# Start columns of the projection weights in their SBUF slots: by tile index instead of by kind

## The chip, the cores and the metric

The kernel runs on one core of one Trainium2 chip. The metric is device time in microseconds (us) for one launch; the time of a kernel is the median of its runs.

## The reference, cut to what matters

One layer of a hybrid block on 528 tokens (16 meta tokens and 512 real ones), width 2048, all in float32:

```python
hn = rmsnorm(h_res, norm_in_g)
P  = hn @ w_in                      # 2048 x 8320: the combined input projection
Pr, Pc = P[..., :4224], P[..., 4224:]
# Pr, after a token shift: r, k, v, g_r (1024 each) and two low-rank parts (64 each)
y  = delta-rule recurrence over 16 heads of 64 (r, decay, k, v, kk, kk*a)
y_a = (groupnorm(y) + bonus) * silu(g_r)
# Pc: Bg, Cg, hc, g_c (1024 each)
y_b = Bg * causal_conv3(Cg * hc) * silu(g_c)
out = rmsnorm(h_res + concat(y_a, y_b) @ w_out, norm_f_g)[:, 16:]
```

## The kernel before

**Projection.** The 8320 columns of `w_in` are 65 tiles of 128 columns. Each tile has a kind and an index: `lora` (one tile), `k`, `v`, `r`, `g`, `C`, `h`, `B`, `gc` (eight tiles each, index `i` from 0 to 7). `plan` (lines 152 to 159) lists them in the order in which they are computed. The products are made in three passes: activations and weights are each split into a high part in the matmul's reduced format (float32r) and the remainder as a low part, and every product is high x high, then weight-high x activation-low, then weight-low x activation-high. The activations lie in `xh` and `xl`, 16 rows (contraction blocks `kt`) of `LX` = 576 columns each. `steps` (L316 to L329) issues the matmuls: the weights are the stationary operand (128 columns, loaded for each matmul by a separate weight load) and `xh` or `xl` the moving one. The matmuls of all tiles stand on L326, except the first six (L485).

Which columns of the activations stream depends on the kind:

```python
FULL = ((0, 256), (256, L))      # lora, k, v:   256 and 272 columns, L = 528
TAIL = ((14, 272), (272, L))     # r, g, C, h:   258 and 256 columns
REAL = ((META, L),)              # B, gc:        512 columns, META = 16
```

So a tile of FULL or TAIL is 96 matmuls: for each of the four quarters of the contraction (`k4`), 12 of the first range (four `kt`, three passes each) and then 12 of the second. A tile of REAL is 48 matmuls of 512 columns.

**Weight slots.** A half row of a weight tile (1024 columns, 512 KB) is brought by a DMA into `raw`, and `split_w` (L136 to L140) makes two quarters of it: for each quarter ScalarE copies the high part (L138) and VectorE or GpSimd subtracts to give the low part (L139). `parts_of` (L128 to L131) takes a slot of `2 * 512 + 64` = 1088 columns from a pool with tag `hl` and six buffers, and puts the high part at start column `o` and the low part at `o + 512`; so up to 64 columns of a slot are free, and `o` says where in the slot the weights begin. Before, `o` is read from the table `SHIFT` (L78) by kind:

```python
SHIFT = {"lora": 16, "k": 16, "v": 16, "r": 32, "C": 64, "h": 32, "B": 16, "g": 32, "gc": 16, "out": 40}
```

`kind_of` (L133, L134) finds the kind of the tile that a quarter belongs to; the first four tiles are computed together, so their eight half rows stand interleaved.

**Where things lie.** In the built program the six slots begin at bytes 4128 + n x 4352 of a partition, `xh` at 42528 and `xl` at 79392. 4352 bytes are 17 x 256 and a row of `xh` is 2304 = 9 x 256, and all these places leave 32 when divided by 256. So the place of an operand's first column modulo 64 columns (256 bytes) is its column number alone: 0 and 0 for the two ranges of FULL, 14 and 16 for TAIL, 16 for REAL, and `o` for the weights, whatever the slot, the contraction block or the part.

**Order.** TensorE's order is written out by hand: the small matmuls of the recurrence (grams L674, triangular inverses L846 to L905, the chunk loop L947 to L1003) are set between projection matmuls by `fill`, which counts 0.43 ns per moving column and stops at hand-set amounts (`FW`). DMAs are put off by the same clock (`later`). After the last projection tile comes the output projection (L1236, and L1445 for its last piece), whose weights are the moving operand: they go through the same slots at start column 40 (`parts_of("out", ...)` in `split_unit`, L1204 to L1216).

Of the kernel before, what the change touches and what calls it, by code (L numbers as in the profile page):

```python
# [74 lines left out]


LX = 576
SHIFT = {"lora": 16, "k": 16, "v": 16, "r": 32, "C": 64, "h": 32, "B": 16, "g": 32, "gc": 16, "out": 40}  # L78


@with_exitstack
def hymba_kernel(ctx: ExitStack, tc: tile.TileContext, xt, xtok, front, w_in, w_out, pv, lup, cst, msk, gf, out):
# [27 lines left out]
    plan = [("lora", 0), ("k", 0), ("r", 0), ("B", 0), ("v", 0), ("k", 1), ("r", 1), ("v", 1), ("g", 0), ("g", 1)]  # L110
# [10 lines left out]
    N_IN = len(stream)  # L121
# [5 lines left out]

    def parts_of(kind, name):  # L128
        t = wp.tile([P, 2 * 512 + 64], F32R, tag="hl", name=name, bufs=6)
        o = SHIFT[kind]  # L130
        return t[:, o : o + 512], t[:, o + 512 : o + 1024]  # L131

    def kind_of(j):  # L133
        return "out" if j >= N_IN else plan[j % 4 if j < 8 else j // 2][0]  # L134

    def split_w(q, rq, eng):  # L136
        hi, lo = parts_of(kind_of(q // 2), f"w{q}")
        nc.scalar.copy(hi, rq)  # L138
        low[q] = eng.tensor_tensor(out=lo, in0=rq, in1=hi.bitcast(F32), op=ALU.subtract).ins  # L139
        quarters[q] = (hi, lo)  # L140
# [90 lines left out]
    for n in range(4):  # L231
        quarters[2 * n] = parts_of(kind_of(n), f"w{2 * n}")
    F0, F1, F2 = KT + P + L, 4 * P + L, 8 * P + 2 * L
    fr = [view("bt", F0), view("r0", 3 * P), view("bk", F1), view("gt0", F2)]
    o = 0
# [61 lines left out]
    with tc.issue_after(head):  # L297
        nc.vector.tensor_scalar(
            out=omm, in0=pvt[:, V_MU : V_MU + 33], scalar1=-1.0, scalar2=1.0, op0=ALU.mult, op1=ALU.add
        )  # L300
        for d, off in (
# [4 lines left out]
                out=d, in0=pvt[:, off : off + 8], scalar1=0.5, scalar2=None, op0=ALU.mult  # L306
            )
        nc.vector.tensor_scalar(
            out=hv[:, 4], in0=pvt[:, V_KA : V_KA + 8], scalar1=-0.5, scalar2=1.0, op0=ALU.mult, op1=ALU.add
# [854 lines left out]
    U = {unit: u for u, unit in enumerate(units)}  # L1164
# [34 lines left out]
    def split_unit(unit, t, home=None):  # L1199
        for q in range(2):  # L1200
            rq = t()[:, q * 512 : (q + 1) * 512]
            if home is None:
                hi, lo = parts_of("out", f"o{U[unit]}_{q}")
            else:  # L1204
                hi, lo = home[q]
            nc.scalar.copy(hi, rq)
            last = nc.vector.tensor_tensor(out=lo, in0=rq, in1=hi.bitcast(F32), op=ALU.subtract)  # L1207
            right[unit, q] = (hi, lo)
        if unit[:2] == (1, "M3"):
            last_low[unit[2]] = last.ins  # L1210

    def here(t, n):
        return xa[t][:, n * 512 : (n + 1) * 512] if n < 2 else xb[n - 2][:, t]
# [83 lines left out]
    def split_home(g):  # L1297
        f = ("S1", "S3", "S4", "S5")[g]
        tiles = [
            pw.tile([P, 4, HT], F32R, tag=f"{f}0{a}", name=f"home{g}{a}").rearrange("p a b -> p (a b)") for a in range(2)  # L1300
        ]
        split_unit(
            (1, "M2", g), passing(1, 1, 0, g),
            [(tiles[0][:, 512 * q : 512 * q + 512], tiles[1][:, 512 * q : 512 * q + 512]) for q in range(2)],
        )
# [7 lines left out]
    for half in range(2):  # L1313
        o = 28 * half
        for g in range(4):
            b = o + 4 + 4 * g
            if half == 0:
                if g == 3:
                    at(-1, begin_chain, 0, g)
                    at(0, split_unit, (0, "M1", g), chained(g))  # L1320
            else:
                at(o + g - 4, begin_chain, 1, g)
                at(o + g - 2, split_unit, (1, "M1", g), chained(g))
            at(max(o + g, b - 5), add_by_transfer, half, 0, 1, g)
            at(b - (6 if g else 5), request, half, 0, 1, g)
            at(b - (4 if g else 5), request, half, 1, 1, g)
            at(b - 2, split_unit, (half, "P5", g), chained(g))
            at(b - 1, add, passing(half, 0, 1, g), half, 1, 1, g)
            at(b - 1, split_unit, (half, "M7", g), passing(half, 0, 1, g))
            at(b, split_unit, (half, "M3", g), passing(half, 1, 1, g))  # L1330
            at(b, add, chained(g), half, 1, 1, g)
            at(b + 1, split_unit, (half, "Q6", g), chained(g))
            at(b + 2, add_by_transfer, half, 1, 0, g)
            at(U[half, "P4", g] - 2, split_unit, (half, "P4", g), chained(g))
            if half == 0:
                at(U[half, "M2", g] - 4, request, 0, 1, 0, g)
                at(U[half, "M2", g] - 2, split_unit, (0, "M2", g), passing(0, 1, 0, g))
            else:
                at(o + 13 + 2 * g, request, 1, 1, 0, g)
# [28 lines left out]
    for u, unit in enumerate(units):  # L1368
        half, prod, g = unit
# [53 lines left out]
    with tc.manual_schedule(engines={mybir.EngineType.DVE, mybir.EngineType.Activation, mybir.EngineType.Pool}):  # L1423
# [16 lines left out]
        for part in range(2):  # L1440
            cols = slice(256 * part, 256 * part + 256)
            for jj in range(8):
                hi, lo = right[(1, "M2", jj // 2), jj % 2]
# [4 lines left out]
            h = here(1, 2)[:, cols]  # L1448
# [70 lines left out]
```

## Time and profile before

| | |
|---|---|
| time, median of 3 runs | 1005.52 us (1004.9 to 1005.81) |
| span of the profiled execution, first to last instruction | 1003.4 us |
| TensorE matmuls busy | 992.7 us (99%), 9723 records |
| TensorE weight loads busy | 914.6 us (91%) |
| VectorE / ScalarE / GpSimd busy | 681.1 / 394.9 / 272.1 us |
| matmuls of L326, busy | 755.2 us, 5470 records |
| granted TensorE clock, mean | 0.998 |

The page of the profile gives shares of the whole span. The chain of waits follows the work that ended last back through time, and merges what stands together on one line: a row is the start in us, the length in us, the engine, the tile, the line and the count. Because consecutive matmuls overlap in the records, a matmul's own duration (some 280 ns) is not what it costs; the step from one start to the next is, and a row of the chain divided by its count gives that step.

### The profile page before, as it was taken

Reading aid. Unit: us, or ns where it says so; the run is one execution under the profiler, and the core shown is the slowest. Engines: PE = TensorE matmul, PEld = TensorE weight load, DVE = VectorE, ACT = ScalarE, POOL = GpSimd, SP = SyncE. Lnnn points to the kernel's source line nnn. Section 1 sums busy time; section 2 is a strip of 40 time slices with the busy share of each in tenths; the row PEclk is TensorE's granted clock in tenths of the full one; section 3 lists DMA queues with packets and bytes.
Section 4 is the critical chain, followed back from the end, with each engine's and each line's share of the span. In section 5 each row is a group of like instructions: output and inputs, shape, how many; then the busy total and the mean of one; then the engine's idle time right before and its main releaser. Section 6 shows DMA issues by size and latency. Waiting matters only on the chain.

```text
span 1003.4 us, 23673 instructions
## 1 busy us (share of the span) xinstructions
PE 992.7 (99%) x9723; PEld 914.6 (91%) x9723; DVE 681.1 (68%) x1247; ACT 394.9 (39%) x729; POOL 272.1 (27%) x284
## 2 busy tenths in 40 slices
PE   9999999999999999999999999999999999999996
PEld 8999999999998999998999998989889898788885
DVE  6777866587765569655569654245554597997897
ACT  7553423344323434323434322223232435546453
POOL 0122524233232323232423223223332333001001
PEclk9999999999999999999999999999999999999999
DMA  9525485546665364864263855968674688797654
GB/s 322 153 90 148 122 222 147 163 122 148 162 167 170 102 166 94 221 163 119 85 171 98 219 148 162 324 204 247 201 228 93 178 267 211 187 299 191 159 127 168
DMA packets 185036, 174.82 MB, mean 174 GB/s; under 512 B 121568, under 2 KB 142816, under 8 KB 184416
## 3 DMA queue, kind: packets, MB, share of 16 engines
q1 hardware_dynamic: 182336, 164.40, 57.0%
q0 software_dynamic: 2304, 8.39, 4.9%
q8 instruction: 76, 1.25, 0.5%
q10 hardware_dynamic: 288, 0.52, 0.1%
q14 instruction: 32, 0.26, 0.1%
HBM read 136.92 MB, written 36.35 MB: 173 GB/s over the span
## 4 chain that ended last, share of the span: by engine, by line
PE 91%; DVE 5%; issue 1%; DMA 1%; ACT 0%; POOL 0%; DVEq 0%; SPq 0%; ACTq 0%; POOLq 0%
PE ps_h L326 9%; PE ps_k L326 9%; PE ps_v L326 9%; PE ps_g L326 9%; PE ps_C L326 9%; PE ps_r L326 9%; PE ps_B L326 9%; PE ps_gc L326 9%; PE M L1236 5%; PE P L1236 2%; PE g L674 2%; DVE o L1207 2%; PE Q L1236 1%; PE ps_lora L326 1%; PE zs L999 1%
## 5 line engine op out<-in xcount | busy, mean ns | idle before, releaser
L139 POOL TENSOR_TENSOR w<-wr,w 128x512 fp32r<-128x512 f32 x119 | 172.2, 1447 | 360.9 <-ACT w L138 305.1
L138 ACT CAST w<-wr 128x512 fp32r<-128x512 f32 x252 | 153.2, 618 | 289.0 <-PE ps_C L326 48.7
L139 DVE TENSOR_TENSOR w<-wr,w 128x512 fp32r<-128x512 f32 x133 | 98.5, 746 | 104.4 <-ACT w L138 104.0
L326 PE MATMUL ps_k<-xh,w 128*128 128x256 f32 (+1 forms) x512 | 96.1, 285 | 0.0
L326 PE MATMUL ps_r<-xh,w 128*128 128x258 f32 (+1 forms) x512 | 95.1, 281 | 0.0
L326 PE MATMUL ps_v<-xh,w 128*128 128x272 f32 (+1 forms) x512 | 94.9, 284 | 0.0
L326 PE MATMUL ps_h<-xh,w 128*128 128x256 f32 (+1 forms) x512 | 94.6, 283 | 0.0
L326 PE MATMUL ps_C<-xh,w 128*128 128x256 f32 (+1 forms) x512 | 93.2, 281 | 0.0
L326 PE MATMUL ps_g<-xh,w 128*128 128x256 f32 (+1 forms) x512 | 92.1, 281 | 0.0
L326 PE MATMUL ps_B<-xh,w 128*128 128x512 f32 x256 | 83.5, 395 | 0.0
L326 PE MATMUL ps_gc<-xh,w 128*128 128x512 f32 x256 | 81.6, 393 | 0.0
L326 PEld LDWEIGHTS ps_k<-xh,w 128*128 128x128 f32 x512 | 80.4, 190 | 0.5
L326 PEld LDWEIGHTS ps_h<-xh,w 128*128 128x128 f32 x512 | 79.6, 188 | 1.3 <-issue 0.6
L326 PEld LDWEIGHTS ps_r<-xh,w 128*128 128x128 f32 x512 | 80.1, 188 | 0.3
L326 PEld LDWEIGHTS ps_v<-xh,w 128*128 128x128 f32 x512 | 79.9, 189 | 0.3
L326 PEld LDWEIGHTS ps_C<-xh,w 128*128 128x128 f32 x512 | 79.2, 188 | 0.6
L326 PEld LDWEIGHTS ps_g<-xh,w 128*128 128x128 f32 x512 | 79.1, 189 | 0.3
L326 PE MATMUL ps_k<-xl,w 128*128 128x256 f32 (+1 forms) x256 | 72.8, 284 | 0.0
L326 PE MATMUL ps_v<-xl,w 128*128 128x256 f32 (+1 forms) x256 | 72.6, 284 | 0.0
L326 PE MATMUL ps_h<-xl,w 128*128 128x258 f32 (+1 forms) x256 | 71.9, 281 | 0.5 <-issue 0.5
L326 PE MATMUL ps_g<-xl,w 128*128 128x258 f32 (+1 forms) x256 | 72.3, 282 | 0.0
L326 PE MATMUL ps_r<-xl,w 128*128 128x258 f32 (+1 forms) x256 | 72.0, 281 | 0.0
(321 smaller groups left out, 2258.9 us busy)
## 6 DMA issues: line engine op xcount, KB each, us to landing
wr<-in_w_in_dram SPq DMA_DIRECT2D x126, 512.0 KB
ct<-opd SPq DMA_DIRECT2D x64, 288.0 KB
wo<-in_w_out_dram SPq DMA_DIRECT2D x24, 512.0 KB
x<-in_w_out_dram POOLq DMA_DIRECT2D x16, 512.0 KB, 6.0
opd<-ar SPq DMA_DIRECT2D x8, 576.0 KB
opd<-gt SPq DMA_DIRECT2D x16, 288.0 KB
opd<-bt SPq DMA_DIRECT2D x64, 64.0 KB
x<-in_w_out_dram SPq DMA_DIRECT2D x8, 512.0 KB
```

The lines of the kernel that those rows point to most:

```text
L138: nc.scalar.copy(hi, rq)
L139: low[q] = eng.tensor_tensor(out=lo, in0=rq, in1=hi.bitcast(F32), op=ALU.subtract).ins
L326: nc.tensor.matmul(ps[r], ww[:, w], xx[:, kt, a:b], start=(kt == 0 and n == 0), stop=(kt == KT - 1 and n == 2))
L674: nc.tensor.matmul(z[h][:, c - c0], bk[hs, c, h : h + 2, :].rearrange("p a s -> p (a s)"), ar[hs, c].rearrange("p a s -> p (a s)"), start= ...
L999: nc.tensor.matmul(d[hs, j], w, x[hs], start=(a == 0), stop=(a == b - 1))
L1207: last = nc.vector.tensor_tensor(out=lo, in0=rq, in1=hi.bitcast(F32), op=ALU.subtract)
L1236: nc.tensor.matmul(bank[s], left(prod, jj, m, s), w, start=(jj == 0 and n == 0), stop=(jj == 7 and n == 2))
```

## The change

The table `SHIFT` goes. The start column is now worked out from kind and index: 40 for the output projection and 16 for `lora`, as before, and `8 * i` for every other tile, so 0, 8, 16, ... 56 columns for index 0 to 7 whatever the kind. `kind_of` returns the pair of kind and index, and the call in `split_unit` passes such a pair. Slots, buffers, instructions and their sizes stay.

```diff
-SHIFT = {"lora": 16, "k": 16, "v": 16, "r": 32, "C": 64, "h": 32, "B": 16, "g": 32, "gc": 16, "out": 40}
+OUT_SHIFT = 40
+
+
+def shift_of(what, i):
+    return OUT_SHIFT if what == "out" else 16 if what == "lora" else 8 * i
...
     def parts_of(kind, name):
         t = wp.tile([P, 2 * 512 + 64], F32R, tag="hl", name=name, bufs=6)
-        o = SHIFT[kind]
+        o = shift_of(*kind)
         return t[:, o : o + 512], t[:, o + 512 : o + 1024]
 
     def kind_of(j):
-        return "out" if j >= N_IN else plan[j % 4 if j < 8 else j // 2][0]
+        return ("out", 0) if j >= N_IN else plan[j % 4 if j < 8 else j // 2]
...
-                hi, lo = parts_of("out", f"o{U[unit]}_{q}")
+                hi, lo = parts_of(("out", 0), f"o{U[unit]}_{q}")
```

## Prediction

> **What bounds the kernel now.** I read the page's busy shares first, then the waits of TensorE, then the table by stage, then the chain of waits.
>
> ```profile
> span 1003.4 us, 23673 instructions
> ...
> PE 992.7 (99%) x9723; PEld 914.6 (91%) x9723; DVE 681.1 (68%) x1247; ACT 394.9 (39%) x729; POOL 272.1 (27%) x284
> ...
> PE 91%; DVE 5%; issue 1%; DMA 1%; ACT 0%; POOL 0%; DVEq 0%; SPq 0%; ACTq 0%; POOLq 0%
> ```
>
> ```profile
> PE pwarm L187 <- DVE cold L184: 1.4, 1, 1.4
> PE ps_h L326 <- issue: 0.5, 1, 0.5
> PE M L1236 <- DVE o L1207: 0.5, 1, 0.5
> ```
>
> The second fence has what TensorE waited for (us in total, times, longest): its three longest waits sum to 2.4 us, and it is otherwise occupied; 91% of the chain is its own. Nothing else can move the time much, unless it makes TensorE wait. Next, L326 alone by stage (us, PE busy and count, PEld busy and count, granted clock, DMA share, GB/s):
>
> ```profile
> 0.00:54.00 54.00, 46.29 (x331) 43.30 (x332) 1.00 0.69 230
> 54.00:619.00 565.00, 522.92 (x3985) 499.75 (x3984) 1.00 0.56 147
> 619.00:842.00 223.00, 186.02 (x1154) 162.92 (x1152) 1.00 0.72 220
> ```
>
> Those are 5470 projection matmuls at full clock. One nanosecond more on each step from start to start is 5.5 us, so a few per cent of a step decide here. The chain gives the steps (start, length, tile, count); these tiles run without anything between them:
>
> ```profile
> 271.34 11.20 PE ps_C L326 x96
> 282.54 11.31 PE ps_h L326 x96
> ...
> 383.30 11.54 PE ps_v L326 x96
> ...
> 619.32 11.38 PE ps_C L326 x96
> ...
> 830.65 10.90 PE ps_gc L326 x48
> ```
>
> Two things are to be seen. A `gc` tile's 512-column matmuls take 10.90 / 48 = 227.1 ns, which is 0.4435 ns a column; by that rate 256, 258 and 272 columns would take 113.5, 114.4 and 120.6, a TAIL tile 48 x 227.9 = 10.94 us and a FULL tile 48 x 234.1 = 11.24. `C`, `h` and `v` take 0.26 to 0.44 and 0.30 more: the short matmuls have an excess. And the same `C` work takes 11.20 at one place and 11.38 at another, so the excess isn't fixed by the size alone. Where it sits, the timeline shows (low-part steps, three matmuls apart):
>
> ```profile
> 271.30 0.28 PE L326 MATMUL ps_C<-xl,w 128*128 128x258 f32 x1
> ...
> 272.38 0.28 PE L326 MATMUL ps_C<-xl,w 128*128 128x258 f32 x1
> ...
> 272.73 0.28 PE L326 MATMUL ps_C<-xl,w 128*128 128x256 f32 x1
> ...
> 273.75 0.28 PE L326 MATMUL ps_C<-xl,w 128*128 128x256 f32 x1
> ...
> 384.63 0.29 PE L326 MATMUL ps_v<-xl,w 128*128 128x272 f32 x1
> ...
> 385.75 0.29 PE L326 MATMUL ps_v<-xl,w 128*128 128x272 f32 x1
> ```
>
> Nine steps each: 1.08 / 9 = 120.0 ns for 258 columns, 1.02 / 9 = 113.3 for 256, 1.12 / 9 = 124.4 for 272. Two columns cost `C` 6.7 ns. What else differs between its two ranges is where the moving columns begin: 14 and 272 (16 modulo 64), against weights that begin at 64 (0). The first is the only kind of range in this projection that doesn't begin a whole number of 16 columns from its weights.
>
> **The change part by part.** The built programs have the same instructions in the same order with the same waits on all engines; only the start columns of the weights differ. Nothing is issued, queued or moved past another. Eight of 65 tiles keep their column (`lora`; `k2`, `v2`, `B2`, `gc2` at 16; `r4`, `g4`, `h4` at 32); 57 move. Of the moving start minus weight start, modulo 64: before, 48 for both FULL ranges; 46 and 48 for `r`, `g`, `h`; 14 and 16 for `C`; 0 for `B`, `gc`. After: -8i for FULL, 14 - 8i and 16 - 8i for TAIL, 16 - 8i for REAL. For odd i (32 tiles) all that was a whole number of 16 columns apart is now 8 off.
>
> *Writers.* ScalarE and the two subtracting engines write to the new columns:
>
> ```profile
> L138 ACT CAST w<-wr 128x512 fp32r<-128x512 f32 x252 | 153.2, 618 | 289.0 <-PE ps_C L326 48.7
> L139 DVE TENSOR_TENSOR w<-wr,w 128x512 fp32r<-128x512 f32 x133 | 98.5, 746 | 104.4 <-ACT w L138 104.0
> ```
>
> I cost this at nothing: ScalarE is idle 289 us before these copies alone, and TensorE does not wait for them. Without that cover, 1% of 618 ns on 252 copies would be 1.6 us.
>
> *Odd i, second TAIL range* (`r`, `g`, `C`, `h`; 16 tiles of 48 matmuls). `h` at 11.31 us less 48 x 120 ns for its first range leaves 115.6 ns a step. From below, the price is -2.1 (down to 113.5); from above, the worst step near it is the 272-column one, 3.8 over its rate, or this:
>
> ```profile
> 989.45 5.91 PE L1445 MATMUL end<-home,m 128*128 128x256 f32 x48
> ```
>
> 48 matmuls of 256 columns in 5.91 us, less one 0.28 for the last, by 47: 120 ns, and `C`'s off-grid range is 120 too. I take that: +4.4 ns x 768 = **+3.4 us**.
>
> *Odd i, first FULL range* (`k`, `v`; 8 tiles). `v` at 240.4 ns a pair less 124.4 leaves 116.0; to 120 is +4.0 x 384 = **+1.5 us** (from below -2.5 x 384 = -1.0). The 272-column range I leave at 124.4: it streams 7.1 ns longer than 256 and already carries an excess; ends -3.8 and, by `C`'s +6.7, +6.7 ns on 384 (-1.5, +2.6 us).
>
> *Starts that now coincide.* In the built program both operands of L1445 begin at the same place modulo 64 columns, and it is the slow 256-column row above. After the change that holds for `k0`, `v0` (i = 0) and the second range of `r2`, `g2`, `C2`, `h2`: 96 x 4.0 + 192 x 4.4 = **+1.2 us**.
>
> *First TAIL range.* It stays off the grid of 16 for every i; 120.0 in `C`: **0**, with ends of -5.6 (to its rate) and +4.4 (to the 124.4 of the slowest steps shown) on 29 moved tiles x 48: -7.8, +6.1 us.
>
> *512 columns* (`B`, `gc`). At its rate when undisturbed, and the other 48-matmul tiles agree; the load of the next weights has twice the time to finish: **0**, from below 0. From above, the early `B` tile among short matmuls:
>
> ```profile
> 51.71 1.40 PE ps_B L326 x6
> ```
>
> 233.3 ns, +6.2 x 8 odd tiles x 48 = +2.4 us. Even i otherwise: **0**; distances of 16 and 48 occur before, and 32 keeps the grid.
>
> The sum is 3.4 + 1.5 + 1.2 = +6.1 us on a span of 1003.4, 1009.5; the median of the runs stands 2.1 above that span, so **1011.6 us**.
>
> A rule of the Trainium skill speaks against all of it. SBUF — State Buffer, section "SBUF: two separate sides", says that on the engine side only the port pair shared by VectorE and GpSimd contends, and that TensorE has its own ports and never waits for anyone. By that rule a start column has no price and the sum is 0; that is the first rival below. The trace doesn't bear it out well, as far as reading alone goes: the same 96 `C` matmuls took 11.20 and 11.38 us. In the Trainium skill too, TensorE: Matmul & The Clock Gate, section "LDWEIGHTS (loading the stationary operand)", gives columns / 1.2 ns, an estimated 107 ns for 128 columns; by it a 256-column step of 113.3 hides the load with 6 ns to spare, and 512 columns hide it easily, which is the side that I took above without it.
>
> **The rivals.** *No change: the start column is not what matters.* The two `C` rows have the same columns and differ by 0.18 us, so the state in which TensorE enters a tile also sets the step; if that is all, 57 moved tiles change nothing: **1005.5**. Against: the 120.0 and 113.3 ns alternate inside one tile, exactly with the range.
>
> *Faster: the excess is a lock between the stream of moving columns and the load of the next weights, which the new columns break.* Before, each tile of a kind meets the same distance, 48 for 41 of 49 short-matmul tiles. If 8 columns off is the better distance, the odd tiles fall to the rate: 16 TAIL tiles x (11.31 - 10.94) + 8 FULL x (11.54 - 11.24) = 8.3 us. Half of that is more likely, since `C`'s first range, off the grid, is not at its rate: 4.2 us, **1001.4**. For: `C` at 16 apart is faster than `h` at 48. It decides if the odd TAIL tiles run under 11.31.
>
> *Slower still.* The off-grid price also falls on the first TAIL range and on 512 columns: +6.1 and +2.4 on top of 6.1, **1020.1**. For: the 233 ns row. Against: the load is hidden there.
>
> That the change doesn't do what it says is excluded by the built programs.
>
> **How the numbers follow.** Forecast 1011.6: 0.45; no change: 0.17; faster: 0.25; slower still: 0.13. A measurement of this kernel can tell about 0.2%, 2 us, from no change. So faster 0.25, same 0.17, slower 0.58. The range runs from 1000, which takes in half of the odd tiles' excess and a little of the first ranges, to 1017, which takes in the upper ends of the FULL 272-column range (+2.6) and of 512 columns (+2.4); left out are the full gain and most of the slower-still case.
>
> **What would show it.** TensorE still without waits, and the writers at 618 and some 690 to 746 ns. Uninterrupted odd TAIL tiles (`C1`, `h1`, `C3`, `C7`, `h7`) at 11.5 us or more in the chain, with 256-column steps near 120; `C2` above `C4`; `gc7` and `B7` at 10.90. The first would be wrong if odd tiles run at or under 11.31; the second if `C2` stays at 11.20; the third if `gc7` leaves 10.90. If the span moves by more than the sum of the L326 steps, the reason lies elsewhere.

## The result, and the profile after

The changed kernel takes **1013.34 us** (median of 4 runs, 1012.58 to 1013.85) where the kernel before takes 1005.21 (median of 4, 1003.84 to 1005.81): a ratio of 1.0082, interval 1.0067 to 1.0096. It is slower by 8.1 us; 1011.6 was forecast. In the code after, the matmuls of `steps` stand on L331 (before: L326), the copies of `split_w` on L143 and L144.

The page of the kernel after: span, busy shares, and the chain's shares by engine.

```profile
span 1011.7 us, 23673 instructions
...
PE 1001.0 (99%) x9723; PEld 920.1 (91%) x9723; DVE 684.9 (68%) x1247; ACT 394.9 (39%) x729; POOL 271.8 (27%) x284
...
PE 92%; DVE 5%; issue 1%; DMA 0%; ACT 0%; POOL 0%; DVEq 0%; ACTq 0%; POOLq 0%
```

Same instructions, 8.3 us more span, 8.3 us more busy TensorE. Its waits (us in total, times, longest) are the three of before to 0.1 us:

```profile
PE pwarm L192 <- DVE cold L189: 1.4, 1, 1.4
PE ps_h L331 <- issue: 0.5, 1, 0.5
PE M L1241 <- DVE o L1212: 0.4, 1, 0.4
```

So no wait was added. The table by stage, for the projection matmuls alone over the whole span, first before, then after (us, PE busy and count, PEld busy and count, granted clock, DMA share, GB/s):

```profile
0.00:1020.00 1020.00, 755.23 (x5466) 705.98 (x5466) 1.00 0.62 171
```

```profile
0.00:1020.00 1020.00, 763.06 (x5466) 711.09 (x5466) 1.00 0.62 171
```

The line's 5466 matmuls carry 7.8 of the 8.3 us, at the same granted clock and DMA load; the rest lies mostly between the small matmuls of the chunk loop (L947 to L1003 before), whose steps are 0.6 us longer though their columns did not change. (There are 5466 records, not 5470: the prediction's three windows count four matmuls that straddle a border twice.) The writers of the weights kept their durations (618 ns before and after on ScalarE, 746 and 750 on VectorE):

```profile
L143 ACT CAST w<-wr 128x512 fp32r<-128x512 f32 x252 | 153.2, 618 | 299.7 <-PE ps_C L331 54.8 <-PE ps_k L331 48.3 <-PE ps_gc L331 41.2
L144 DVE TENSOR_TENSOR w<-wr,w 128x512 fp32r<-128x512 f32 x133 | 98.9, 750 | 107.6 <-ACT w L143 100.6 <-DMA d<-sg 6.3 <-DMA ct<-opd 0.4
```

What grew is read in the chain of after (start, length, tile, count): `C0` at 132.54, `C1` at 272.29, `v5`, `C2` at 423.81, `C4` at 624.43, `h7`, `B7`, `gc7`.

```profile
132.54 11.38 PE ps_C L331 x96
...
272.29 11.37 PE ps_C L331 x96
283.66 11.41 PE ps_h L331 x96
...
385.69 11.77 PE ps_v L331 x96
...
423.81 11.47 PE ps_C L331 x96
...
624.43 11.41 PE ps_C L331 x96
...
815.94 11.44 PE ps_h L331 x96
827.38 11.20 PE ps_B L331 x48
838.58 11.21 PE ps_gc L331 x48
```

`C1` went from 11.20 to 11.37, `h1` from 11.31 to 11.41, `v5` from 11.54 to 11.77, and the 512-column tiles from 10.90 to 11.20 and 11.21: 227.1 ns a matmul became 233.4. `C0` rose too, from

```profile
132.30 11.20 PE ps_C L326 x96
```

to 11.38, though its start goes from 64 to 0 and so keeps its place modulo 64 (the prediction counts it among the moved tiles); `e3_c_at_0` and `e8_tail_at_64` come back to this. Inside `C1`, in the timeline of after:

```profile
272.25 0.28 PE L331 MATMUL ps_C<-xl,w 128*128 128x258 f32 x1
...
273.32 0.28 PE L331 MATMUL ps_C<-xl,w 128*128 128x258 f32 x1
...
273.67 0.28 PE L331 MATMUL ps_C<-xl,w 128*128 128x256 f32 x1
...
274.72 0.28 PE L331 MATMUL ps_C<-xl,w 128*128 128x256 f32 x1
```

Nine steps each: 1.07 / 9 = 118.9 ns for 258 columns (120.0 before), 1.05 / 9 = 116.7 for 256 (113.3 before). To have every tile, including those that other work interrupts, I summed all steps from one matmul's start to the next in the timeline, by range, and took after minus before:

| range | after minus before, us |
|---|---|
| first of TAIL, 258 columns | -1.08 |
| second of TAIL, 256 columns | +4.03 |
| first of FULL (`k`, `v`), 256 columns | +0.71 |
| second of FULL, 272 columns | +1.51 |
| REAL, 512 columns | +2.99 |
| `lora` (columns unchanged) | -0.40 |
| sum | +7.75 |

The tiles that keep their column are a control: `k2`, `v2`, `B2`, `gc2`, `r4`, `g4` and `h4` changed by 0.04 us at most. Only `lora` moved, by -0.40, and it lies 0.2 to 0.7 us under this profile of before in all the other runs too, so that row is not the change's.

### The profile page after: what moved, and what is told of

It is laid out like the page before. It is cut to its first block, busy times and chain, and to the rows that moved or that the text cites. A ratio compares the mean times of both kernels' runs of the same rounds, so it can differ in the third digit from the quotient of the medians.

```text
span 1011.7 us, 23673 instructions
## 1 busy us (share of the span) xinstructions
PE 1001.0 (99%) x9723; PEld 920.1 (91%) x9723; DVE 684.9 (68%) x1247; ACT 394.9 (39%) x729; POOL 271.8 (27%) x284
## 4 chain that ended last, share of the span: by engine, by line
PE 92%; DVE 5%; issue 1%; DMA 0%; ACT 0%; POOL 0%; DVEq 0%; ACTq 0%; POOLq 0%
PE ps_k L331 9%; PE ps_v L331 9%; PE ps_h L331 9%; PE ps_C L331 9%; PE ps_g L331 9%; PE ps_r L331 9%; PE ps_B L331 9%; PE ps_gc L331 9%; PE M L1241 5%; PE P L1241 2%; PE g L679 2%; DVE o L1212 2%; PE Q L1241 1%; PE ps_lora L331 1%; PE zs L1004 1%
## 5 line engine op out<-in xcount | busy, mean ns | idle before, releaser
L144 POOL TENSOR_TENSOR w<-wr,w 128x512 fp32r<-128x512 f32 x119 | 171.7, 1444 | 368.0 <-ACT w L143 315.9
L143 ACT CAST w<-wr 128x512 fp32r<-128x512 f32 x252 | 153.2, 618 | 299.7 <-PE ps_C L331 54.8
L144 DVE TENSOR_TENSOR w<-wr,w 128x512 fp32r<-128x512 f32 x133 | 98.9, 750 | 107.6 <-ACT w L143 100.6
L331 PE MATMUL ps_k<-xh,w 128*128 128x256 f32 (+1 forms) x512 | 97.2, 286 | 0.0
L331 PE MATMUL ps_v<-xh,w 128*128 128x272 f32 (+1 forms) x512 | 96.1, 285 | 0.0
L331 PE MATMUL ps_r<-xh,w 128*128 128x258 f32 (+1 forms) x512 | 95.7, 282 | 0.0
L331 PE MATMUL ps_h<-xh,w 128*128 128x256 f32 (+1 forms) x512 | 95.2, 284 | 0.0
L331 PE MATMUL ps_C<-xh,w 128*128 128x256 f32 (+1 forms) x512 | 94.2, 282 | 0.0
L331 PE MATMUL ps_g<-xh,w 128*128 128x256 f32 (+1 forms) x512 | 92.7, 281 | 0.0
L331 PE MATMUL ps_B<-xh,w 128*128 128x512 f32 x256 | 84.5, 398 | 0.0
L331 PE MATMUL ps_gc<-xh,w 128*128 128x512 f32 x256 | 82.7, 397 | 0.0
L331 PEld LDWEIGHTS ps_k<-xh,w 128*128 128x128 f32 x512 | 80.7, 189 | 0.5
L331 PEld LDWEIGHTS ps_h<-xh,w 128*128 128x128 f32 x512 | 79.7, 188 | 1.4 <-issue 0.6
L331 PEld LDWEIGHTS ps_r<-xh,w 128*128 128x128 f32 x512 | 80.2, 188 | 0.3
L331 PEld LDWEIGHTS ps_v<-xh,w 128*128 128x128 f32 x512 | 80.2, 188 | 0.3
L331 PEld LDWEIGHTS ps_C<-xh,w 128*128 128x128 f32 x512 | 79.6, 188 | 0.6
L331 PEld LDWEIGHTS ps_g<-xh,w 128*128 128x128 f32 x512 | 79.0, 188 | 0.3
L331 PE MATMUL ps_k<-xl,w 128*128 128x256 f32 (+1 forms) x256 | 73.0, 285 | 0.0
L331 PE MATMUL ps_v<-xl,w 128*128 128x256 f32 (+1 forms) x256 | 72.8, 284 | 0.0
L331 PE MATMUL ps_h<-xl,w 128*128 128x258 f32 (+1 forms) x256 | 72.0, 281 | 0.5 <-issue 0.5
L331 PE MATMUL ps_g<-xl,w 128*128 128x258 f32 (+1 forms) x256 | 72.2, 282 | 0.0
L331 PE MATMUL ps_C<-xl,w 128*128 128x258 f32 (+1 forms) x256 | 72.1, 282 | 0.0
```

The source lines that it names most:

```text
L331: nc.tensor.matmul(ps[r], ww[:, w], xx[:, kt, a:b], start=(kt == 0 and n == 0), stop=(kt == KT - 1 and n == 2))
```

## The experiments

**The theory** after the result: what counts is the *distance*, the start of the moving columns minus the start of the weights, modulo 64 columns, because the stream of moving columns and the load of the next weights get in each other's way. **Rivals**: the weights' own start column (its alignment) sets the price; or the result hangs on the way in which TensorE enters a tile, and the columns are only what disturbs it.

Times below are medians against runs of the kernel before on the same chip; "steps" are sums as in the table above, minus before.

### Both operands moved by 8: `e1_x8_w8`

```diff
-SHIFT = {"lora": 16, "k": 16, "v": 16, "r": 32, "C": 64, "h": 32, "B": 16, "g": 32, "gc": 16, "out": 40}
+SHIFT = {"lora": 24, "k": 24, "v": 24, "r": 40, "C": 8, "h": 40, "B": 24, "g": 40, "gc": 24, "out": 40}
...
-    xh = xp.tile([P, KT, LX], F32R, name="xh")
-    xl = xp.tile([P, KT, LX], F32R, name="xl")
+    xh = xp.tile([P, KT, LX], F32R, name="xh")[:, :, 8:]
+    xl = xp.tile([P, KT, LX], F32R, name="xl")[:, :, 8:]
```

> The kernel before with xh and xl begun 8 columns later in their rows and every projection weight begun 8 columns later too (C at 8, which is 64 + 8 modulo 64). Theory D (the step goes by the distance between moving start and weight start, modulo 64 columns): all distances are those of before, so the time is that of before, 1005.2, L326 steps as before (C tile 11.20, v 11.54, gc 10.90). Theory W (the weights' own place, on or off a multiple of 16 columns, sets the price): all projection weights are now off, so more than the changed kernel paid, about +10 to +14 us, gc near 11.2. Theory M (the moving operand's own place): a change too, sign open.

Measured: 1005.84 against 1005.31, ratio 1.0005 (0.9996 to 1.0015). Every operand's own place moved by 8 columns, every distance stayed, and the time stayed within 0.15%. The chain has `gc7` and `h1` as before; `C0` and `C1`, though, rose to 11.38:

```profile
271.23 11.38 PE ps_C L326 x96
282.61 11.30 PE ps_h L326 x96
...
831.55 10.89 PE ps_gc L326 x48
```

The own place is ruled out for the 512-column tiles and `h`. That two prices cancel here is ruled out too, for 512 columns: `gc3`, whose weights alone go 8 columns on in the change (16 to 24), went from 227.3 to 233.2 ns a step, the next run moves the other operand alone and pays as well, and here both moved and nothing was paid. The 0.18 us of `C0` and `C1` is the difference that the same tile kind shows inside the kernel before (11.20 and 11.38); it comes here with no distance changed.

### Only the moving operand moved by 8: `e2_x8`

The edit of `xh` and `xl` above, with `SHIFT` as before.

> The kernel before with xh and xl begun 8 columns later, weights at the old table: distances 56 (FULL), 54 and 56 (r, g, h), 22 and 24 (C), 8 (B, gc). Theory D: the steps that the changed kernel showed at those distances (FULL +1.0 and +2.5 ns, second TAIL range +2.9 and C +4.9, first TAIL range -0.5, 512 columns +5.3): about +10 us, 1015. Theory W: as before, 1005.2, since no weight moves. Theory of the grid of 16 from the prediction, 512 columns free of charge: about +6 to +8 us with gc at 10.90.

Measured: 1015.96 against 1005.31, ratio 1.0104 (1.0089 to 1.0119). No weight moved, no writer of weights changed, and it costs more than the change itself: steps +10.7 (the change: +7.75), of which +4.8 on the second TAIL range, +4.1 on 512 columns, +2.3 on 272.

```profile
273.71 11.44 PE ps_C L326 x96
285.15 11.43 PE ps_h L326 x96
...
387.19 11.77 PE ps_v L326 x96
...
841.44 11.21 PE ps_gc L326 x48
```

These are, to 0.07 us, the lengths of the change's tiles (11.37, 11.41, 11.77, 11.21). Together with the run before this settles for the 512-column tiles, `h` and `v` that the price belongs to the distance.

### `C` at column 0: `e3_c_at_0`

```diff
-SHIFT = {"lora": 16, "k": 16, "v": 16, "r": 32, "C": 64, ...
+SHIFT = {"lora": 16, "k": 16, "v": 16, "r": 32, "C": 0, ...
```

> The kernel before with C's weights at column 0 in place of 64, all else as before. If places count modulo 64 columns, nothing changes: 1005.2, C tiles at 11.20 (C1, C2, C3) and 11.38 (C4). If they count modulo more than 64 (128 or 256 columns), C tiles change as in the changed kernel, where C0 at column 0 took 11.38: about +0.5 us over eight tiles.

Measured: 1005.28 against 1005.31, ratio 0.9998 (0.9989 to 1.0007); the `C` and `h` tiles as before:

```profile
271.06 11.20 PE ps_C L326 x96
282.26 11.31 PE ps_h L326 x96
```

64 columns, 256 bytes, further is the same place for `C`. So the rise of `C0` in the change (column 64 to 0) is no price of its distance. (Half of 64 is not a period: in the sweep below 512 columns take 227.9 ns at distance 0 and 232.5 at 32.)

### Only the 512-column tiles by index: `e4_512_by_index`

```diff
-        o = SHIFT[kind]
+        o = 8 * kind[1] if kind[0] in ("B", "gc") else SHIFT[kind[0]]
```

`kind_of` and the call in `split_unit` pass pairs, as in the change.

> The kernel before with B and gc alone by index (8 columns for each), the other kinds by the old table. If the prices of the tiles add up, the 512-column steps of the changed kernel come back here alone: +3.0 us, 1008.2, gc7 and B7 at 11.2 us, C and h tiles as before. If the 512-column price came from the tiles ahead of them (the state in which TensorE enters), gc7 and B7 stay at 10.90 and the time at 1005.2.

Measured: 1007.97 against 1005.31, ratio 1.0026 (1.0015 to 1.0038); steps of 512 columns +3.08, of TAIL and FULL within 0.3.

```profile
281.76 11.31 PE ps_h L326 x96
...
382.86 11.54 PE ps_v L326 x96
...
822.01 11.20 PE ps_B L326 x48
833.21 11.21 PE ps_gc L326 x48
```

`B7` and `gc7` rise alone to what they have after the change; `h1` and `v5` stay. More than a third of the change's loss sits in tiles that I had costed at nothing.

### Only `k` and `v` by index: `e12_k_v_by_index`

The same edit with `("k", "v")`.

> The kernel before with k and v alone by index, the other kinds by the old table. If the prices add up, the steps of the changed kernel come back here: 256 columns +0.9 ns and 272 columns +2 ns on average over 16 tiles, +2.2 us, 1007.4. As the prediction had it: +1.5 us for odd i and +0.4 for k0 and v0, all of it in the 256-column range, 272 columns unchanged at 123.6 to 124.4: 1007.1. The two differ in the range that pays; v5 tile 11.77 by the first, 11.73 with its 272-column step at 124.4 by the second.

Measured: 1007.08 against 1005.38, ratio 1.0016 (1.0007 to 1.0025); steps of the 256-column range +0.78, of the 272-column range +1.44.

```profile
282.58 11.31 PE ps_h L326 x96
...
384.08 11.76 PE ps_v L326 x96
...
832.35 10.90 PE ps_gc L326 x48
```

`v5` takes on its length after the change (11.76 here, 11.77 there); its 272-column steps went from 123.4 to 125.4 ns and its 256-column steps from 117.1 to 119.7. The range that the prediction had left at 124.4 pays most of it. So two of the three parts are the same alone as in the change: 512 columns +3.08 and +2.99, FULL +2.22 and +2.22. The TAIL tiles by index alone were not tried, so that their +2.95 would come alone is not shown.

### The grid shifted by 2, 4 and 6: `e5_8i_plus_2`, `e6_8i_plus_4`, `e7_8i_plus_6`

```diff
-    return OUT_SHIFT if what == "out" else 16 if what == "lora" else 8 * i
+    return OUT_SHIFT if what == "out" else 16 if what == "lora" else 8 * i + 2
```

and 4 and 6, on the changed kernel; one run each, so that every even distance occurs once.

> The changed kernel with every indexed start 2 columns later (8 i + 2), to read the step at the distances in between: 2 columns less than those of the changed kernel. Theory D with a granularity of 8 columns or more: steps near those of the changed kernel, 512 columns at 227 for i = 2 (distance 62) and 232 to 234 elsewhere. Theory D with a finer granularity: other steps, and the cheap distances of 512 columns (0 and 16) gone, about +0.6 us on the changed kernel.

> The same with 4 columns later (8 i + 4). If what counts is whether the distance is a multiple of 16, all indices are off now and every class stays at its dear steps: 512 columns 232 to 234, 256 columns 117 to 120; a span of about 1013 us. A class of cheap distances between the multiples of 8 would show as steps of 227 (512 columns) or under 115 (256 columns).

> The same with 6 columns later (8 i + 6); expectation as for 8 i + 4. With the first TAIL range (14) it now meets the whole multiples of 8: if its 120 ns come from being off the grid of 8, its steps fall at distance 0, 16 or 48 to 115 to 118; if they come from its 258 columns, they stay at 118 to 120.

Measured, each in a single run: 1012.63, 1014.38 and 1013.33, against 1005.21. The offset of the grid matters little; spread over the distances, all are slow. With `8 * i + 4` the tiles `h1` and `gc7`:

```profile
284.68 11.68 PE ps_h L331 x96
...
839.74 11.05 PE ps_gc L331 x48
```

Mean steps of the four kernels with columns by index, by distance modulo 64 (ns; steps that other work lengthens are left out):

| columns | cheapest distances | dearest distances |
|---|---|---|
| 512 | 34: 227.4; 0: 227.9; 60: 228.3; 4: 228.4 | 8, 24, 50, 54: 233.4; 48: 233.5; 40: 234.0 |
| 272 | 48: 123.5; 40: 124.0 | 26: 127.2; five others 126.5 to 126.7 |
| 256 | 42: 115.5; 62: 116.1; 48: 116.4 | 10: 119.8; 4: 119.7; 24: 119.5 |
| 258 | 24: 117.7; 18: 118.1 | 2: 122.7; 32: 124.3, but see below |

A grid of 16, as the prediction had it, is not in this table: 48, a multiple of 16, is among the dearest for 512 columns (0 costs 227.9) and the cheapest for 272, and 258 columns pay some 118 to 120 nearly everywhere. 512 columns are cheap at a few distances and dear at most, and 272 columns have other cheap ones.

The table has a weakness: each distance was met at one tile index of one kernel, so it is mixed with the place in the program. How much that is, tiles of one distance show. For 512 columns it is little: in the kernel before, all at distance 0, 15 of the 16 tiles take 226.6 to 229.0 ns (the early `B0` 230.5), and the dear distances stand clear of that. For 256 columns it is as much as the table's whole range: at distance 16 in the kernel before, `C0` to `C3` take 113.3 and `C4`, `C5` and `C7` 117.8 to 117.9. And the 124.3 of 258 columns at 32 is no price of that distance: `C5` and `h5` take 118.3 and 118.6 there, while `g5`, with the same columns in the same kernel, runs in stretches of 140 ns.

### The low part of the 512-column tiles moved by 8: `e9_low_part_off_8`

```diff
-        return t[:, o : o + 512], t[:, o + 512 : o + 1024]
+        p = o + 520 if kind in ("B", "gc") else o + 512
+        return t[:, o : o + 512], t[:, p : p + 512]
```

This sets apart *which* weights meet the stream. Each `kt` has three passes (high weights, high again, low weights); now only the weights of the third are off, and they are loaded while the second streams.

> The kernel before with only the low part of the B and gc weights begun 8 columns later in its slot; the high part stays at distance 0, the low part goes to 56. The passes are (high weights, xh), (high, xl), (low, xh). Theory L (the moving stream of a matmul meets the load of the weights of the next matmul): the step of the second pass, under which the low part is loaded, becomes dear (233 in place of 227), the other two stay near 227; about +1.5 us, gc7 about 11.0. Theory S (what counts is a matmul's own weights against its own moving columns): the third pass becomes dear. If the high weights' distance alone counts: 1005.2.

Measured: 1008.65 against 1005.16, ratio 1.0036 (1.0023 to 1.005); `gc7` at 11.22, as after the change:

```profile
833.46 11.22 PE ps_gc L327 x48
```

Inside it (`xl` is the second pass), the timeline of this kernel:

```profile
836.33 0.40 PE L327 MATMUL ps_gc<-xl,w 128*128 128x512 f32 x1
836.57 0.62 PE L327 MATMUL ps_gc<-xh,w 128*128 128x512 f32 x2
837.03 0.40 PE L327 MATMUL ps_gc<-xl,w 128*128 128x512 f32 x1
837.27 0.62 PE L327 MATMUL ps_gc<-xh,w 128*128 128x512 f32 x2
837.73 0.40 PE L327 MATMUL ps_gc<-xl,w 128*128 128x512 f32 x1
```

From the second pass to the third 0.24 us, for the other two steps 0.46 together. All 48 steps average 232.0, 239.9 and 228.3 ns by pass (before: 226.0, 227.0, 227.1), and repeat in this order to the end of the tile. The dear step is the one in which the moved weights are loaded, +13 ns; the third pass, which works with them, pays 1. In 15 of the 16 tiles (all but `B0`) the second pass is the dearest, at 235 to 240. That fits the load of the next weights and speaks against the weights in use. Two things it doesn't explain: the +5 ns of the first pass, under which nothing moved is loaded, and the sum. About +1.5 us was expected and +3.5 came (512-column steps +3.54): with one load of three moved, `gc7` is as slow as with all three (11.22 and 11.21). So there is no fixed price for each load at a dear distance.

### `r`, `g`, `h` at 64 like `C`: `e8_tail_at_64`

```diff
-SHIFT = {..., "r": 32, "C": 64, "h": 32, "B": 16, "g": 32, ...
+SHIFT = {..., "r": 64, "C": 64, "h": 64, "B": 16, "g": 64, ...
```

> The kernel before with r, g and h at column 64, C's place (distances 14 and 16), all else as before. Theory D alone: 24 tiles at C's 11.20 us in place of about 11.31: 1002.6. If C's 11.20 came from how TensorE enters the tile (C4 took 11.38 at the same distance), the tiles come out anywhere between 11.20 and 11.40: 1002.6 to 1007.

Measured: 1007.01 against 1005.21, ratio 1.002 (1.0011 to 1.003). If a distance had one price, 24 tiles would have fallen from 11.31 to the 11.20 of `C`, 2.6 us. Instead `h1` rose, and `C1`, whose columns nobody touched, rose with it:

```profile
271.31 11.39 PE ps_C L326 x96
282.70 11.39 PE ps_h L326 x96
```

In the kernel before all 48 steps of `C1`'s first range are 120 ns and all of its second 113 or 114. Here they waver, 116 to 123 in the first range and 117 to 120 in the second, and so they do, in the same numbers, in `C4` of the kernel before. So one distance has two ways of running, a regular one (11.20) and a wavering one (11.38 to 11.39). Distance alone is not the whole of it.

At these distances the wavering way is the usual one. After the change the tiles with index 0 have these distances, and the table above has 119.4 ns for 258 columns at 14 and 117.7 for 256 at 16; here `r`, `g` and `h` average 119.4 and 117.5. The exception is the 113.3 of `C0` to `C3` in the kernel before. What decides between the ways is not shown: here the columns of `r`, `g` and `h` alone changed and `C0` to `C3` left the regular way, in `e10_r_g_h_at_38` below they changed too and `C0` to `C3` kept it, and in `e1_x8_w8` no distance changed and `C0` and `C1` left it. In the change `C0` to `C3` grew by 0.85 us together; leaving the regular way is part of that.

### TAIL tiles at 38: `e10_r_g_h_at_38` and `e11_all_tail_at_38`

From the sweep: at start 38 (distances 40 and 42) a TAIL pair takes 119.2 + 115.5 = 234.7 ns, at 32 (`r`, `g`, `h` in the kernel before) it takes 120.3 + 115.6 = 235.9.

```diff
-SHIFT = {"lora": 16, "k": 16, "v": 16, "r": 32, "C": 64, "h": 32, "B": 16, "g": 32, "gc": 16, "out": 40}
+SHIFT = {"lora": 16, "k": 16, "v": 16, "r": 38, "C": 38, "h": 38, "B": 16, "g": 38, "gc": 16, "out": 40}
```

(`e10_r_g_h_at_38` leaves `C` at 64.)

> The kernel before with r, g and h at column 38 (distances 40 and 42, the cheapest pair met in the probes: 119.2 + 115.4 ns in place of 120.4 + 115.6), C at 64. If the step of a distance holds wherever it is met: -1.3 ns x 48 x 24 tiles = -1.5 us, 1003.8. If the way TensorE enters a tile weighs more (r, g, h at 64 cost +1.8 us and took C's 11.20 away): C off 11.20 by up to 0.2 us a tile, 1005 to 1007.

> As before with r, g, h and C all at column 38. If the step of a distance holds wherever it is met: 234.6 ns a pair for all 32 tiles, 11.26 us a tile, -1.5 us and another -0.1 for C: 1003.6. If entry weighs more: 1005 to 1007, and C tiles equal to h tiles.

Measured: 1003.46 and 1003.22 against 1005.16, ratios 0.9984 (0.9975 to 0.9993) and 0.9981 (0.9972 to 0.999). With `C` at 64 (first fence) `h1` is at 11.20 and `C4` stays at 11.39; with all four at 38 (second fence: `C1`, `h1`, `C4`, `C7`, `h7`) every `C` and `h` tile that the chain shows whole is at 11.20 or 11.21:

```profile
280.66 11.20 PE ps_h L326 x96
...
617.07 11.39 PE ps_C L326 x96
```

```profile
269.75 11.20 PE ps_C L326 x96
280.95 11.20 PE ps_h L326 x96
...
617.38 11.21 PE ps_C L326 x96
...
794.53 11.21 PE ps_C L326 x96
805.73 11.20 PE ps_h L326 x96
```

In the first run `r`, `g` and `h` average 119.1 and 115.5 ns, so here the sweep's prices held where they were met again. Single steps still go up and down (116 to 124 ns in the first range of `C1`), and interrupted tiles such as `C5` average 115.3 in place of 114.2 in the second.

The second run beats both kernels: the one before by 0.19%, and the changed one by 1.0% (the ratio of the two ratios, 1.0082 / 0.9981 = 1.0101; between 1.0077 and 1.0124 from the ends of both intervals).

## Why the prediction was right, and where its sum was not

**The bound** held: no wait came, the writers kept their times, and 7.8 of the span's 8.3 us are longer steps of the projection matmuls. **The mechanism** held: a start column has a price, and its relation to the moving columns sets it; `e1_x8_w8` and `e2_x8` show it. Its form, a grid of 16 columns, did not hold. **The size** came out near through misses of both signs, and that is luck: of the +7.7 us, 3.5 stand in the terms that were priced (at 6.1), and 4.2 net in those put at nothing. The prediction's terms beside the sums of steps:

| term | predicted, us | measured, us |
|---|---|---|
| odd i, second TAIL range | +3.4 | +2.3 |
| odd i, first FULL range | +1.5 | +0.3 |
| coinciding starts (`k0`, `v0`; second range of `r2`, `g2`, `C2`, `h2`) | +1.2 | +0.9 |
| even i, 256-column ranges otherwise | 0 | +1.2 |
| 272 columns | 0 | +1.5 |
| 512 columns | 0 | +3.0 |
| first TAIL range | 0 | -1.1 |
| `lora` | 0 | -0.4 |
| sum | +6.1 | +7.7 |

- *512 columns* is the term that was mis-sized most. "The load of the next weights has twice the time to finish" did not help: 227.1 became 233.4 ns. The upper end taken from the early `B` tile, +6.2 on odd tiles, was the right price by luck, since that tile has distance 0 and pays for something else; and i = 4 and 6 pay it too (233.5 and 232.5 ns; i = 2, at distance 0, stays at 227.9). The sign to watch, `gc7` and `B7` at 10.90, failed.
- *The grid of 16*, from which "odd i" and "even i otherwise: 0" came, fell: even tiles pay, as the table of distances shows.
- *Odd i, FULL*: the base was wrong. The 116.0 ns came from 124.4 for 272 columns, read from one stretch of the timeline in hundredths of a microsecond; over whole tiles `v5` had 123.4 and 117.1 (117.3 to 117.8 in the odd `k`). Nor did all reach the 120 taken from L1445: 117.0 to 119.8 after.
- *272 columns* "already carries an excess" and still took 2 ns more on average (from 123.4 or 123.5 up to 126.6); its upper end held.
- *First TAIL range*: a gain of 1.1, inside the bounds. Being off a grid is not what it pays for; it pays about as much nearly everywhere, also where `e7_8i_plus_6` brings it to multiples of 8 (117.7 to 120.3, leaving out 32, where `g5` has its stretches of 140).
- *Coinciding starts* came right for `C2`, 11.47 against `C4`'s 11.41, but are no special case: 256 columns take 119.2 ns at distance 0 and 119.5 to 119.8 at 4, 10 and 24. Odd TAIL tiles came at 11.37 to 11.45, not the 11.5 named.

That a load has time enough under 512 columns is in the rows of before: each is recorded at 188 ns and begins 3 to 4 ns after a matmul does, so it is over within the 227, and the price came all the same.

```profile
L326 PEld LDWEIGHTS ps_gc<-xh,w 128*128 128x128 f32 x256 | 47.7, 188 | 10.0
```

Under the short matmuls the loads are recorded at 188 to 190 ns, longer than their steps of 113 to 124, and neighbouring records overlap. Loads of 64 columns are recorded at 136:

```profile
L999 PEld LDWEIGHTS zs<-ct 64*64 64x64 f32 x256 | 13.1, 136 | 0.0
```

So 64 columns more take some 52 ns. An estimate from these two rows gives 104 ns for 128 columns, near the prediction's 107, with some 84 on top of it in each record. Whether a step of 113.3 has 6 ns to spare, these rows do not show.

**The rivals.** "No change" falls by the result and by `e2_x8`. Its page, the Trainium skill's SBUF — State Buffer, section "SBUF: two separate sides", has TensorE's port never waiting on anyone. The runs show a delay all the same, and it goes with the distance between TensorE's own two operands (`e2_x8`), while `e1_x8_w8`, where the other engines' accesses moved by the same 8 columns, shows next to none; here the measurement decides. What spoke for this rival, two ways of running at one distance, is real (`e8_tail_at_64`) but worth 0.18 us a tile and no ground for no change. "Faster" was wrong for 8 columns off, but better columns than the old table's exist: with 38 the kernel is 0.19% faster. That this loosens a lock is not shown. "Slower still" was half right: 512 columns paid, the first TAIL range did not.

**Open** stays what makes a distance dear. That the stream and the load of the next weights get in each other's way fits `e9_low_part_off_8` in part and is not shown beyond that. The runs show that 256 bytes more are the same place, the dear step under which the moved weights load, and two ways of running at one distance, but not the rule by which a table of distances could be worked out ahead, nor what decides a tile's way.

## What to carry to other kernels

In this kernel, where TensorE is the bound and each matmul loads new weights, the columns at which weights and moving operand begin were worth about 1%. In one like it, treat them as a tuning parameter: keep their distance one and the same for tiles of one shape, sweep it, and read the step from start to start in tiles that nothing interrupts. A distance that is good for one stream length can be bad for another, and tiles with the same distance can still run at two prices, so the whole is to be timed, not added up from a table. Spare time under a long matmul is no proof that a load beneath it is free.

## What the runs showed of the hardware that was not expected

- 512-column matmuls, 227.1 ns apart at distance 0, took 232 to 234 at some 20 of the 32 even distances, though the loads under them have twice the time of those under 256.
- 64 columns of float32 (256 bytes) more distance changes nothing (`e3_c_at_0`, 1005.28 against 1005.31); 8 columns more cost 1.04% (`e2_x8`).
- In a tile that nothing interrupts the steps can settle into a pattern that repeats with the three passes: 232, 240, 228 ns in `gc7` of `e9_low_part_off_8`, 231, 232, 237 after the change (`gc7` too). With the same columns, `C` runs at 11.20 or at 11.38 us in the kernel before.
